# Seven products for eight: Strassen's scheme in the gate and up projections of two fp32 feed-forwards

## The chip, the cores and the metric
The kernel runs on one core of a Trainium2 chip. The metric is the device time of one execution in microseconds; the figure compared is the median over runs. Arithmetic that has to keep fp32 accuracy is done with each fp32 operand split into a rounded part hi and a remainder lo (both of the matmul type fp32r), and three matmuls per product: hi x hi, hi x lo, lo x hi.

## The reference
512 tokens of width 1024 pass two residual blocks (a pooling mixer with a feed-forward, latent attention with a feed-forward), then a third with differential attention and a mixture of experts. The change concerns the two feed-forwards, of hidden width 2816:

```python
def swiglu(h, w_gate, w_up, w_down):
    return (jax.nn.silu(h @ w_gate) * (h @ w_up)) @ w_down
...
    h = rms_norm(x, norm_ffn[i])
    x = x + swiglu(h, ffn_w_gate[i], ffn_w_up[i], ffn_w_down[i])
```

## The kernel before
The tokens lie along the free axis: x is 8 tiles (KT) of 128 channels x 512 tokens, and stays in SBUF. The hidden width is 22 tiles (FT) of 128. `ffn` (L772) takes the hidden tiles in two halves of 11 (HF). For each hidden tile j it takes one weight of 128 x 2048 from the stream (a *pair*: the gate and the up tile), and for gate and up does 8 x 3 matmuls of 512 columns (`mm3`, L519) into one PSUM bank each, 48 in all. The moving operands xh and xl are x times the norm's gain. The norm's factor per token, R, is not in them: it comes late (two hooks after the first pair's two halves make it on VectorE, GpSimd, TensorE and ScalarE), and `evac` (L781) multiplies both PSUM results by R, applies silu, multiplies, and splits the hidden tile into hh and hl. After 11 pairs, 8 down tiles of 11 x 3 matmuls are added to x. The second half's down tiles also call `after(d)`, which prepares the next stage's norm.

The weights come through `Stream` (L82). A queue of DMAs on the SyncE queue fills raw buffers; `split_part` (L193) rounds one 512-column part to hi on ScalarE, and `flush` (L248) does lo = raw - hi, on VectorE, or on GpSimd for parts 2 and 4 (POOLED). The rings have 3 raw, 3 hi and 2 lo buffers of 128 x 2048 (BUFS, L51); a raw buffer is free when its last part is split, hi and lo when `release` says so. In the feed-forwards the order of the work is that of the code: `pump` (L268), called between groups of matmuls, issues the next part's split if there is room, and every engine executes its own instructions in the order issued. The attention stages are issued by a planner with a cost model; the expert stage's order follows the same way.

Four PSUM banks serve as accumulators (`acc`, L488) in rotation. All other tiles are 57 slots of an arena (`tmp`, L485). The two lines on which a pair rests are:

```python
c = slice(k * 256 + m * P, k * 256 + (m + 1) * P)
self.mm3(ps, wh[:, c], wl[:, c], xh[k], xl[k], k == 0, k == KT - 1)
```

In the profile every operation of the planner's engines stands at its helper's line, L357, so names of tiles tell them apart: acc<-xh,hi is a gate or up matmul, acc<-hh,hi a down matmul, lo<-raw,hi a weight's split, t<-acc,R and u<-acc,R an evacuation.

Of the kernel before, what the change touches and what calls it, by code (L numbers as in the profile page):

```python
# [17 lines left out]
P = 128  # L18
T = 512
NT = T // P  # L20
D = 1024
KT = D // P
FF = 2816
FT = FF // P
HF = FT // 2

# [59 lines left out]
class Stream:  # L86
# [16 lines left out]
    def add(self, ap, arena=False):  # L103
        self.items.append(ap)
        self.arena.append(arena)

# [7 lines left out]
    def load(self):  # L114

        nc, tmp = self.net.nc, self.net.tmp
        while self.loaded < len(self.items):
            i, ap = self.loaded, self.items[self.loaded]
            if i >= self.first:
                if not self.load_piece():  # L120
                    return
                continue
            if not self.arena[i]:
                if not self.spare["raw"] or any(self.arena[self.split:i]):
                    return
# [3 lines left out]
                self.raw[i] = self.cut(t, w)  # L129
            else:  # L130
# [62 lines left out]
    def split_part(self):  # L193
        nc, i = self.net.nc, self.split
        if i >= self.first:
            return self.split_piece()
        if self.part == 0:
# [12 lines left out]
        self.half = lo[:, c], r, hi[:, c], i, last  # L210
        if self.part in POOLED[self.phase]:
            self.flush(nc.gpsimd)
        if last:
            self.part = 0
            self.raw.pop(i)
            self.split += 1

    def split_piece(self):
        nc, i, k = self.net.nc, self.split, self.part
# [48 lines left out]
    def pump(self, n=1):  # L268

        plan = self.net.nc  # L270
        for _ in range(n):
            i = self.split
            if i == len(self.items):
                return
            if i < self.first and i >= self.loaded:
                self.flush()
                self.load()
            got = self.raw.get(i, ())
            if self.part >= len(got):
# [20 lines left out]
    def take(self):  # L300
        i = self.taken
        self.taken += 1
        while self.split <= i:
            self.split_part()
        if self.split == i + 1 and self.part == 0:
            self.flush()
        hi, lo, tags = self.out.pop(i)
        w = hi, lo
        self.held.append((w, tags))
        return w  # L310

    def piece(self):

# [161 lines left out]
class Net:  # L475
# [37 lines left out]
    def mm(self, ps, lhsT, rhs, start=True, stop=True):  # L513
        self.nc.tensor.matmul(ps, lhsT, rhs, start=start, stop=stop)
# [254 lines left out]
        sched.spawn(weights(), 0)  # L769


    def ffn(self, l, hooks, after, extra=None):  # L772

        nc = self.nc
        hooks = list(hooks)
        xh, xl = self.held
        for hf in range(2):
            hh, hl = [], []
            pend = []

            def evac(pg, pu):  # L781
                t, u = self.tmp("t"), self.tmp("u")
                nc.vector.tensor_tensor(t, pg, self.R, op=OP.mult)
                nc.scalar.activation(t, t, AF.Silu)
                nc.vector.tensor_tensor(u, pu, self.R, op=OP.mult)
                nc.vector.tensor_tensor(t, t, u, op=OP.mult)
                hh.append(self.tmp("hh", F32R))
                hl.append(self.tmp("hl", F32R))
                self.hilo(hh[-1], hl[-1], t)

            for j in range(HF):
                wh, wl = self.ws.take()
                pp = []
                for m in range(2):
                    ps = self.acc()
                    for k in range(KT):
                        c = slice(k * 256 + m * P, k * 256 + (m + 1) * P)
                        self.mm3(ps, wh[:, c], wl[:, c], xh[k], xl[k], k == 0, k == KT - 1)
                    pp.append(ps)
                    self.ws.pump(2)  # L800
                    if hooks:
                        hooks.pop(0)()
                    elif extra:
                        next(extra, None)
                self.ws.release()
                pend.append(pp)
                if not hooks:
                    while pend:
                        evac(*pend.pop(0))
            for d in range(KT):  # L810
                wh, wl = self.ws.take()
                ps = self.acc()
                for f in range(HF):
                    c = slice(f * P, (f + 1) * P)
                    self.mm3(ps, wh[:, c], wl[:, c], hh[f], hl[f], f == 0, f == HF - 1)
# [5 lines left out]
                if hf == 1:  # L821
                    after(d)

    def ffn_weights(self, l, arena=0):
        for hf in range(2):
            for j in range(HF):
                self.ws.add(self.a["ffn_gu"][l, hf * HF + j], hf * HF + j < arena)
            for d in range(KT):
                self.ws.add(self.a["ffn_dn"][l, hf, d])


    def rope_tables(self):
# [1286 lines left out]
def _host(inp):  # L2119

    f = np.ascontiguousarray
    o = {}
    x = inp["x"][0]
# [5 lines left out]
    def twice(v):  # L2129
# [12 lines left out]
    o["ffn_gu"] = f(gu.reshape(2, 2, KT, P, FT, P).transpose(1, 4, 3, 2, 0, 5)  # L2142
                    .reshape(2, FT, P, 2048))
    o["ffn_dn"] = f(inp["ffn_w_down"].reshape(2, 2, HF, P, KT, P).transpose(0, 1, 4, 3, 2, 5)
                    .reshape(2, 2, KT, P, HF * P))

    wd = inp["mla_w_down"][0]
    wd = np.concatenate([wd, wd[:, 512:]], axis=1)
# [26 lines left out]
    r = np.arange(P)  # L2175
# [4 lines left out]
    c = np.arange(T)[None, :] - 3 * P - r[:, None]  # L2180
# [10 lines left out]
    b = np.zeros((P, 4, 384), np.float32)  # L2191
# [47 lines left out]
```

## Time and profile before

| | |
|---|---|
| median of 3 runs | 1550.54 us (1550.25 to 1555.14) |
| the profiled execution's own time | 1551.3 us |
| its span | 1549.5 us |
| TensorE busy | 1502.5 us, 97% |
| VectorE busy | 946.9 us, 61% |
| ScalarE busy | 753.2 us, 49% |
| GpSimd busy | 397.6 us, 26% |
| weight loads by SyncE's queue | 201.03 MB of 221.57 MB moved |

The two feed-forwards take the stretches from about 36 to 402 us and from about 580 to 945 us; attention, between and after them, and the experts to the end. Busy shares are means over these stages. A matmul's duration in a row is its way through the array, so neighbours overlap: the pace of TensorE is the distance between starts. VectorE's operations overlap a little too. A row's time on GpSimd is rough.

### The profile page before, as it was taken

How to read it: one execution, taken by the hardware profiler on the slowest of the kernel's cores; microseconds unless marked ns; L12 is line 12 of the kernel's file. 1: busy time of each engine (PE TensorE's matmuls, PEld its weight loads, DVE VectorE, ACT ScalarE, POOL GpSimd, SP SyncE). 2: the span in 40 equal slices, each digit the busy share in tenths (PEclk: the TensorE clock that was granted, in tenths of full speed). 3: DMA queues.
4: the chain of work that ended last, by engine and by line, in shares of the span. 5: the costliest groups of instructions: out<-in, count | busy, mean ns of one | idle time of the engine just before them, and what ended most of it. 6: DMA issues, size and time to landing. Idle time of an engine off the chain costs nothing.

```text
span 1549.5 us, 21142 instructions
## 1 busy us (share of the span) xinstructions
PE 1502.5 (97%) x7697; PEld 1222.4 (79%) x7697; DVE 946.9 (61%) x1672; ACT 753.2 (49%) x1553; POOL 397.6 (26%) x314
## 2 busy tenths in 40 slices
PE   8999999999999999999999999999979799999996
PEld 7788888888878888888888889999968666666664
DVE  6464334445387855443444466888986487878774
ACT  5323213223266743232223244787784277777774
POOL 3322123221242113221232123222312222222221
PEclk9999999999999999999999999999979799999999
DMA  6121232223210214313322232212038799999981
GB/s 243 62 104 61 95 135 84 99 73 113 80 63 7 90 62 142 109 57 109 120 97 86 75 111 86 78 57 95 27 112 297 223 312 357 368 366 373 366 295 29
DMA packets 69931, 221.57 MB, mean 143 GB/s; under 512 B 7616, under 2 KB 16960, under 8 KB 56640
## 3 DMA queue, kind: packets, MB, share of 16 engines
q1 hardware_dynamic: 56448, 201.03, 36.5%
q0 software_dynamic: 4064, 14.16, 3.9%
q10 hardware_dynamic: 9312, 5.01, 1.1%
q8 instruction: 61, 1.00, 0.3%
q14 instruction: 46, 0.38, 0.1%
HBM read 208.63 MB, written 11.53 MB: 142 GB/s over the span
## 4 chain that ended last, share of the span: by engine, by line
PE 88%; DVE 5%; ACT 4%; DMA 2%; issue 1%; POOL 0%; ACTq 0%; POOLq 0%; SPq 0%; DVEq 0%
PE acc L357 76%; PE pss L357 8%; PE pst L357 4%; ACT p L357 1%; DVE x L357 1%; DMA bnd<-bands 1%; DVE p L357 1%; DVE xl L357 0%; DVE lo L357 0%; DMA out<-ring,idx 0%; DMA raw<-ffn_gu 0%; ACT hi L357 0%; ACT kl L357 0%; ACT wh L357 0%; ACT kh L357 0%
## 5 line engine op out<-in xcount | busy, mean ns | idle before, releaser
L357 POOL TENSOR_TENSOR lo<-raw,hi 128x512 fp32r<-128x512 f32 (+1 forms) x157 | 224.6, 1440 | 695.9 <-ACT hi L357 593.9
L357 PE MATMUL acc<-xh,hi 128*128 128x512 f32 x744 | 290.5, 390 | 0.5 <-ACT xh L357 0.5
L357 PE MATMUL acc<-xl,hi 128*128 128x512 f32 x744 | 289.6, 389 | 0.3 <-DVE xl L357 0.3
L357 PE MATMUL acc<-xh,lo 128*128 128x512 f32 x744 | 289.5, 389 | 0.0
L357 ACT ACTIVATE hi<-raw 128x512 fp32r<-128x512 f32 (+1 forms) x378 | 208.8, 607 | 86.2 <-issue 59.8
L357 DVE TENSOR_TENSOR wl<-raw,wh 128x512 fp32r<-128x512 f32 x288 | 203.0, 748 | 53.0 <-ACT wh L357 46.8
L357 DVE TENSOR_TENSOR lo<-raw,hi 128x512 fp32r<-128x512 f32 (+1 forms) x221 | 216.5, 989 | 19.8 <-ACT hi L357 19.1
L357 ACT ACTIVATE wh<-raw 128x512 fp32r<-128x512 f32 x320 | 177.5, 621 | 0.0
L357 PEld LDWEIGHTS acc<-xh,hi 128*128 128x128 f32 x744 | 139.7, 188 | 29.8 <-ACT xh L357 0.9
L357 PEld LDWEIGHTS acc<-xl,hi 128*128 128x128 f32 x744 | 139.7, 188 | 29.3 <-DVE xl L357 0.6
L357 PEld LDWEIGHTS acc<-xh,lo 128*128 128x128 f32 x744 | 139.6, 188 | 29.0
L357 DVE TENSOR_TENSOR u<-acc,R 128x512 f32<-128x512 f32 x44 | 30.4, 691 | 181.0 <-PE acc L357 181.0
L357 PE MATMUL acc<-hh,hi 128*128 128x512 f32 x352 | 136.9, 389 | 0.0
L357 PE MATMUL acc<-hl,hi 128*128 128x512 f32 x352 | 136.9, 389 | 0.0
L357 PE MATMUL acc<-hh,lo 128*128 128x512 f32 x352 | 136.9, 389 | 0.0
L357 ACT ACTIVATE hh<-t 128x512 fp32r<-128x512 f32 x44 | 27.8, 632 | 218.4 <-DVE t L357 218.4
L357 DVE TENSOR_TENSOR x<-acc,x 128x512 f32<-128x512 f32 x59 | 40.4, 689 | 119.0 <-PE acc L357 118.9
L357 PE MATMUL acc<-hi,xh 128*128 128x256 f32 x384 | 111.4, 290 | 0.0
L357 PE MATMUL acc<-lo,xh 128*128 128x256 f32 x384 | 109.2, 284 | 0.6 <-DVE lo L357 0.6
L357 PE MATMUL acc<-hi,xl 128*128 128x256 f32 x384 | 109.0, 284 | 0.0
L357 PE MATMUL acc<-wh,teh 128*96 128x512 f32 x224 | 103.1, 460 | 0.2 <-ACT teh L357 0.2
L357 PE MATMUL acc<-wl,teh 128*96 128x512 f32 x224 | 88.1, 393 | 0.8 <-DVE wl L357 0.8
(319 smaller groups left out, 2851.9 us busy)
## 6 DMA issues: line engine op xcount, KB each, us to landing
raw<-moe_w SPq DMA_DIRECT2D x200, 256.0 KB, 8.0
raw<-moe_w SPq DMA_DIRECT2D x46, 1024.0 KB, 11.1
raw<-ffn_gu SPq DMA_DIRECT2D x43, 1024.0 KB, 4.9
raw<-ffn_dn SPq DMA_DIRECT2D x32, 704.0 KB, 4.1
raw<-da_in SPq DMA_DIRECT2D x12, 1024.0 KB, 4.8
raw<-mla_up SPq DMA_DIRECT2D x4, 832.0 KB, 4.4
raw<-mla_o_a SPq DMA_DIRECT2D x12, 256.0 KB, 3.8
raw<-da_o_a SPq DMA_DIRECT2D x12, 256.0 KB, 2.9
```

Source lines behind the costliest of these rows:

```text
L357: r = f(*args, **kw)
```

## The change
Per layer, pairs 0 to 3 stay plain (`plain`) and evacuate as before; from pair 4 on every third is plain on normalized operands (`later`); the other 12 are *summed pairs* (`mixed`). A summed pair computes gate and up for both halves of the tokens at once. With the channels cut into even and odd tiles and the tokens into halves of 256 (H), eight block products become seven of sums (the Winograd form of Strassen's scheme). Each product is 4 x 3 matmuls of 256 columns; two products share a PSUM bank, and VectorE adds the seven results to two hidden halves.

The weight's sums are made in `split_mixed`: of the four 512-column quarters p, q, r, s of the raw tile it needs p, q, p-r side by side with r+s and the like. GpSimd makes two of the four sums and VectorE two; ScalarE rounds seven quarters in four operations, and VectorE subtracts in four (1024, 512, 512 and 1536 columns). The results lie in two groups of hi and lo buffers (products 0 to 3, and 4 to 6). The tokens' sums are made in `mixed_x`, a generator of 4 blocks with 6 steps each, two channel tiles a block: e and o (x times gain times R), their hi and lo, the sums t and e, and their hi and lo. Steps are issued between the matmuls of pairs 1 to 3: two blocks in pair 1, one in the first half of pair 2, one in pair 3.

The hidden tiles are taken in three sets of 8, 7 and 7, with 8 down tiles each, so x is added to three times. Rings: 2 raw, 3 hi, 3 lo. The arrays of weights are laid out anew on the host for this (even before odd tiles). Attention and experts keep their code.

```diff
-HF = FT // 2
+SETS = ((0, 8), (8, 15), (15, 22))
+PLAIN = 4
+EVERY = 3
+H = T // 2
-BUFS = {"raw": 3, "hi": 3, "lo": 2}
+BUFS = {"raw": 2, "hi": 3, "lo": 3}
...
+    def split_mixed(self):
...
+        if step == 0:
+            self.both = self.net.tmp("rs")
+            pool.tensor_tensor(self.both, r, s, op=OP.add)
+            hi(0, 2, pq)
+        elif step == 1:
+            lo(0, 2, pq)
+            pool.tensor_tensor(r, p, r, op=OP.subtract)
+        elif step == 2:
+            hi(3, 1, self.both)
+        elif step == 3:
+            dve.tensor_tensor(p, self.both, p, op=OP.subtract)
+            lo(3, 1, self.both)
+            self.both = None
+        elif step == 4:
+            hi(2, 1, p)
+            dve.tensor_tensor(q, q, p, op=OP.subtract)
+        elif step == 5:
+            lo(2, 1, p)
+            self.ready.append(self.group)
+        elif step == 6:
+            hi(0, 3, qrs)
+        else:
+            lo(0, 3, qrs)
+            self.ready.append(self.group)
...
+    def mixed_x(self, l, full, parts):
...
+        for i in range(KT // 2):
+            e, o, t = self.tmp("xe"), self.tmp("xo"), self.tmp("xt")
+            normed(e, 2 * i)
+            normed(o, 2 * i + 1)
+            yield
+            even, odd = self.pair("b"), self.pair("b")
+            diff(t[:, a], e[:, b], e[:, a], pool)
+            rounded(even[0], e)
+            rounded(odd[0], o)
+            yield
+            diff(t[:, b], o[:, b], t[:, a], pool)
+            diff(even[1], e, even[0].bitcast(F32))
+            diff(odd[1], o, odd[0].bitcast(F32))
+            yield
+            diff(e[:, b], o[:, b], e[:, b])
+            diff(e[:, a], o[:, a], t[:, b])
...
+            for n, (h, c) in enumerate(((even, a), (odd, a), (t12, b), (t12, a), (odd, b),
+                                        (t34, b), (t34, a))):
+                parts[n].append((h[0][:, c], h[1][:, c]))
...
+        def mix_some(n):
+            for _ in range(n):
+                if not hooks and (last or steps[0] < 18):
+                    next(mix, None)
+                    steps[0] += 1
...
+            def product(n, out):
+                nonlocal got
+                if n in (0, 4):
+                    got = self.ws.take_group(n == 4)
+                c = (n % 4) * T
+                for i, (bh, bl) in enumerate(parts[n]):
+                    k = slice(c + i * P, c + (i + 1) * P)
+                    self.mm3(out, got[0][:, k], got[1][:, k], bh, bl, i == 0, i == KT // 2 - 1)
...
+                self.ws.pump()
...
+                if n == 1:
+                    nc.scalar.activation(s1, bank[0], AF.Copy)
+                    add(g0, s1, bank[1])
+                elif n == 3:
+                    add(s0, s1, bank[2])
+                    add(g1, s0, bank[3])
+                    self.ws.pump()
+                elif n == 5:
+                    add(s1, g1, bank[5])
+                    add(g1, g1, bank[4])
+                    add(s0, s0, bank[5])
+                    nc.scalar.activation(g, g, AF.Silu)
+            add(s0, s0, bank[6])
+            nc.vector.tensor_tensor(g, g, s, op=OP.mult)
+            hidden(g)
```

Two engines show how the instructions move at the start of the first layer.

VectorE, from the evacuation of pair 1 on. Before, evacuations and splits alternate, with steps of the rope tables (ang, k) between:

```order
L357 TENSOR_TENSOR t<-acc,R 128x512
L357 TENSOR_TENSOR u<-acc,R 128x512
L357 TENSOR_TENSOR t<-t,u 128x512
L357 TENSOR_TENSOR hl<-t,hh 128x512
L357 TENSOR_TENSOR lo<-raw,hi 128x512
L357 TENSOR_SCALAR k<-ang 128x512
L357 TENSOR_TENSOR lo<-raw,hi 128x512
```

Now there come after the same evacuation block 2 of the normalized tiles (xe, xo, bl), then the first group of pair 4's weight (its lo of 1024 columns, then its sums and their lo):

```order
L447 SCALAR_TENSOR_TENSOR xe<-x,vecs,R 128x512
L447 SCALAR_TENSOR_TENSOR xo<-x,vecs,R 128x512
L447 TENSOR_TENSOR bl<-xe,bh 128x512
L447 TENSOR_TENSOR bl<-xo,bh 128x512
L447 TENSOR_TENSOR xe<-xo,xe 128x256
L447 TENSOR_TENSOR xe<-xo,xt 128x256
L447 TENSOR_TENSOR bl<-xt,bh 128x512
L447 TENSOR_TENSOR bl<-xe,bh 128x512
L447 TENSOR_TENSOR lo<-raw,hi 128x1024
L447 TENSOR_TENSOR raw<-rs,raw 128x512
L447 TENSOR_TENSOR lo<-rs,hi 128x512
```

Behind these stand one more sum and its lo, the evacuation of pair 2 (t, u, t, hl), a lo of 1536 columns (pair 4's second group), and only then block 3 with the same eight rows, the evacuation of pair 3, and the first lo of pair 5. The order in the second layer is the same.

GpSimd at the same place. Before, it has lo splits of parts 2 and 4, and three small things for the rope tables:

```order
L357 TENSOR_TENSOR lo<-raw,hi 128x512
L357 CAST ident_b<-ident 128x128
L357 CAST mask_b<-causal 128x128
L843 DMA pos<-positions 128x512
L357 TENSOR_TENSOR lo<-raw,hi 128x512 x58
```

Now the token sums of block 2 (xt), pair 4's two weight sums, then those of block 3 and of pair 5:

```order
L447 TENSOR_TENSOR xt<-xe 128x256
L447 TENSOR_TENSOR xt<-xo,xt 128x256
L447 TENSOR_TENSOR rs<-raw 128x512
L447 TENSOR_TENSOR raw<-raw 128x512
L447 TENSOR_TENSOR xt<-xe 128x256
L447 TENSOR_TENSOR xt<-xo,xt 128x256
L447 TENSOR_TENSOR rs<-raw 128x512
L447 TENSOR_TENSOR raw<-raw 128x512
```

So pair 4's weight sums stand before the last block's token sums on GpSimd, and pair 5's right behind them; the rope tables' work comes after both.

On TensorE 24 pairs of 48 matmuls become 24 of 84, in seven runs of twelve. In all 2016 matmuls of 256 columns stand in place of 1152 of 512.

## Rows read from the trace of the kernel before
**Rows 1.** The page, its first part: busy time, share of the span, instructions.
```profile
PE 1502.5 (97%) x7697; PEld 1222.4 (79%) x7697; DVE 946.9 (61%) x1672; ACT 753.2 (49%) x1553; POOL 397.6 (26%) x314
```
**Rows 2.** The chain in order of time, both feed-forwards: start us, us, what.
```profile
51.09 348.21 PE acc L357 x1536
...
591.61 353.59 PE acc L357 x1581
```
**Rows 3.** Windows, a stretch of the first feed-forward: us, each engine's busy, PEclk, DMA.
```profile
100.00:150.00 50.00, 50.00 (x222) 41.41 (x221) 25.56 (x32) 15.07 (x27) 12.30 (x9) 1.00 0.26 86
```
**Rows 4.** Timeline of TensorE, differential attention: start us, us, instruction; first and last.
```profile
964.89 0.28 PE L357 MATMUL acc<-hi,xl 128*128 128x256 f32 x1
...
973.28 0.28 PE L357 MATMUL acc<-lo,xh 128*128 128x256 f32 x1
```
**Rows 5.** Timeline of VectorE, start of the first feed-forward; idle and releaser in brackets.
```profile
51.76 0.69 DVE L357 TENSOR_TENSOR t<-acc,R 128x512 f32<-128x512 f32 x1 [6.95 <-ACT R L357]
...
55.70 0.68 DVE L357 TENSOR_TENSOR lo<-raw,hi 128x512 fp32r<-128x512 f32 x1
...
62.38 0.68 DVE L357 TENSOR_TENSOR t<-acc,R 128x512 f32<-128x512 f32 x1
62.98 0.68 DVE L357 TENSOR_TENSOR u<-acc,R 128x512 f32<-128x512 f32 x1
...
65.77 0.69 DVE L357 TENSOR_TENSOR lo<-raw,hi 128x512 fp32r<-128x512 f32 x1
66.37 1.52 DVE L357 TENSOR_SCALAR k<-ang 128x512 f32<-128x512 f32 x1
67.81 1.78 DVE L357 TENSOR_TENSOR lo<-raw,hi 128x512 fp32r<-128x512 f32 x1
```
**Rows 6.** Timeline of VectorE, pooling mixer: a scalar_tensor_tensor and the next start.
```profile
28.61 0.74 DVE L357 SCALAR_TENSOR_TENSOR x<-acc,vecs,x 128x512 f32<-128x512 f32 x1
29.27 0.74 DVE L357 SCALAR_TENSOR_TENSOR xl<-x,vecs,xh 128x512 fp32r<-128x512 f32 x1
```
**Rows 7.** Groups by line and form: operation, count, busy us, mean ns, idle before.
```profile
L357 DVE TENSOR_TENSOR t<-t,u 128x512 f32<-128x512 f32 x44 | 30.5, 693 | 5.7 <-ACT t L357 1.3
...
L357 DVE TENSOR_TENSOR on<-acc,on 128x256 f32<-128x256 f32 x16 | 6.7, 419 | 7.4 <-ACT on L357 7.3
...
L357 ACT ACTIVATE hi<-raw 128x512 fp32r<-128x512 f32 x342 | 194.6, 620 | 86.2 <-issue 59.8 <-PE acc L357 15.8 <-DMA raw<-ffn_dn 5.5
...
L357 POOL TENSOR_TENSOR lo<-raw,hi 128x512 fp32r<-128x512 f32 x153 | 222.6, 1465 | 686.0 <-ACT hi L357 584.0 <-PE acc L357 66.9 <-issue 21.3
...
L357 POOL TENSOR_TENSOR lo<-raw,hi 128x128 fp32r<-128x128 f32 x4 | 2.0, 501 | 9.9 <-ACT hi L357 9.9
```
**Rows 8.** DMA issues: KB each, median us from issue to landing.
```profile
raw<-ffn_gu SPq DMA_DIRECT2D x43, 1024.0 KB, 4.9
```
**Rows 9.** Timelines of GpSimd and of VectorE beside it, first feed-forward.
```profile
66.25 2.80 POOL L357 TENSOR_TENSOR lo<-raw,hi 128x512 fp32r<-128x512 f32 x2 [5.68 <-ACT hi L357]
...
141.54 3.01 POOL L357 TENSOR_TENSOR lo<-raw,hi 128x512 fp32r<-128x512 f32 x2 [8.15 <-ACT hi L357]
...
141.96 1.43 DVE L357 TENSOR_TENSOR lo<-raw,hi 128x512 fp32r<-128x512 f32 x1 [0.27 <-ACT hi L357]
143.65 0.69 DVE L357 TENSOR_TENSOR t<-acc,R 128x512 f32<-128x512 f32 x1 [0.26 <-PE acc L357]
```
**Rows 10.** Windows, end of the differential attention, columns as in rows 3.
```profile
1130.00:1135.00 5.00, 3.06 (x14) 2.79 (x15) 3.55 (x13) 4.11 (x11) 0.00 (x0) 0.75 0.00 0
...
1140.00:1145.00 5.00, 1.62 (x7) 1.09 (x7) 4.31 (x12) 4.85 (x12) 0.70 (x1) 0.77 0.51 157
1145.00:1150.00 5.00, 3.83 (x17) 3.05 (x16) 3.24 (x11) 5.00 (x15) 0.00 (x0) 0.50 0.01 2
1150.00:1155.00 5.00, 4.36 (x14) 3.85 (x14) 4.89 (x13) 4.97 (x13) 1.28 (x1) 0.50 0.72 211
```

More of the change, by code (lines that the diff above doesn't have):

```diff
@@ L101, in __init__, with add @@
         self.hold, self.gate, self.phase = False, None, 0
-    def add(self, ap, arena=False):
+        self.mixed, self.group, self.both, self.ready = {}, None, None, []
+    def add(self, ap, arena=False, mixed=False):
+        if mixed:
+            self.mixed[len(self.items)] = None
         self.items.append(ap)
@@ L216, in split_part, with group, hi, lo @@
             self.split += 1
+    def group(self, i):
+        th, tl = self.room()
+        return self.tile("hi", F32R, th), self.tile("lo", F32R, tl), (th, tl)
+    def split_mixed(self):
+        nc, i, step = self.net.nc, self.split, self.part
+        dve, pool = nc.vector, nc.gpsimd
+        if step == 0:
+            self.flush()
+            if i >= self.loaded:
+                self.load()
+        if step in (0, 6):
+            self.group = self.room()
+            self.group = (self.tile("hi", F32R, self.group[0]),
+                          self.tile("lo", F32R, self.group[1]), self.group)
+        p, q, r, s = self.raw[i]
+        t = self.mixed[i]
+        def hi(k, n, src):
+            c = slice(k * self.PART, (k + n) * self.PART)
+            nc.scalar.activation(self.group[0][:, c], src, AF.Copy)
+        def lo(k, n, src):
+            c = slice(k * self.PART, (k + n) * self.PART)
+            dve.tensor_tensor(self.group[1][:, c], src, self.group[0][:, c].bitcast(F32),
+                              op=OP.subtract)
+        pq, qrs = t[:, :2 * self.PART], t[:, self.PART:4 * self.PART]
+        self.part += 1
+        if step == 0:
+            self.both = self.net.tmp("rs")
[21 more added lines that the diff above has]
+            self.ready.append(self.group)
+            self.group = None
+            self.raw.pop(i)
+            self.mixed[i] = None
+            self.split += 1
+            self.flushed += 1
+            self.spare["raw"] += 1
+            self.part = 0
+            self.load()
     def split_piece(self):
@@ L278, in pump @@
             got = self.raw.get(i, ())
+            if i in self.mixed:
+                if not got or self.part in (0, 6) and not self.room():
+                    return
+                self.split_part()
+                continue
             if self.part >= len(got):
@@ L310, in take, with take_group @@
         return w
+    def take_group(self, last):
+        while not self.ready:
+            self.split_part()
+        hi, lo, tags = self.ready.pop(0)
+        self.held.append(((hi, lo), tags))
+        self.taken += last
+        return hi, lo
     def piece(self):
@@ L776, in ffn @@
         xh, xl = self.held
[L777 to L793, printed above, removed]
-                for m in range(2):
[L795 to L800, printed above, removed]
+        parts = [[] for _ in range(7)]
@@ new lines, in ffn, with plain, mm @@
+        steps = [0]
+        def plain(last):
+            wh, wl = self.ws.take()
+            pp = []
+            def mm(m, k, begin, end):
+                o = (2 * m + k % 2) * T + k // 2 * P
+                c = slice(o, o + P)
+                self.mm3(pp[m], wh[:, c], wl[:, c], xh[k], xl[k], begin, end)
+            def mix_some(n):
[3 more added lines that the diff above has]
+                        steps[0] += 1
+            if last:
+                pp += [self.acc(), self.acc()]
+                for k in range(KT):
+                    for m in range(2):
+                        mm(m, k, k == 0, k == KT - 1)
+                    xh[k] = xl[k] = None
+                    if k > 1:
+                        mix_some(1)
+                    if k % 2:
+                        self.ws.pump(2)
+            else:
+                for m in range(2):
+                    pp.append(self.acc())
+                    for n, k in enumerate((0, 2, 4, 6, 1, 3, 5, 7)):
+                        mm(m, k, n == 0, n == KT - 1)
+                        if n % 4 < 3:
+                            mix_some(1)
+                    self.ws.pump(3)
@@ L801, in ffn, with hidden @@
                     if hooks:
                         hooks.pop(0)()
-                    elif extra:
-                        next(extra, None)
[L805 to L809, printed above, removed]
+            self.ws.release()
+            pend.append(pp)
+            if not hooks:
+                while pend:
+                    evac(*pend.pop(0))
+        def hidden(t):
+            hh.append(self.tmp("hh", F32R))
+            hl.append(self.tmp("hl", F32R))
+            self.hilo(hh[-1], hl[-1], t)
@@ new lines, in later @@
+        def later():
+            wh, wl = self.ws.take()
+            pp = []
+            for m in range(2):
+                ps = self.acc()
+                for n, k in enumerate((0, 2, 4, 6, 1, 3, 5, 7)):
+                    o = (2 * m + k % 2) * T + k // 2 * P
+                    c = slice(o, o + P)
+                    self.mm3(ps, wh[:, c], wl[:, c], *full[k], n == 0, n == KT - 1)
+                    if n % 2:
+                        self.ws.pump()
+                pp.append(ps)
+            self.ws.release()
+            t = self.tmp("t")
+            nc.scalar.activation(t, pp[0], AF.Silu)
+            nc.vector.tensor_tensor(t, t, pp[1], op=OP.mult)
+            hidden(t)
@@ L810, in ffn @@
+        for f0, f1 in SETS:
+            hh.clear()
+            hl.clear()
+            for j in range(f0, f1):
+                if j < PLAIN:
+                    plain(j == PLAIN - 1)
+                    if j == PLAIN - 1:
+                        for _ in mix:
+                            pass
+                elif self.plain(j):
+                    later()
+                else:
+                    mixed()
             for d in range(KT):
@@ L812, in ffn @@
                 ps = self.acc()
-                for f in range(HF):
+                n = f1 - f0
+                for f in range(n):
                     c = slice(f * P, (f + 1) * P)
-                    self.mm3(ps, wh[:, c], wl[:, c], hh[f], hl[f], f == 0, f == HF - 1)
+                    self.mm3(ps, wh[:, c], wl[:, c], hh[f], hl[f], f == 0, f == n - 1)
                     if f % 3 == 1:
```

73 lines of the change are left out of this document (65 added, 8 removed).

## The prediction
> **What bounds the kernel now.** I read the page first: TensorE is busy 97% of the span, VectorE 61%, ScalarE 49%, GpSimd 26% [rows 1]. Then the chain of waits in order of time: it runs through the first feed-forward as one piece of 348.21 us with 1536 matmuls and through the second as one of 353.59 us with 1581 [rows 2]. Nothing is waited for in either, so only less TensorE work or a new wait can move these stages. 348.21 / 1536 gives 226.7 ns for a 512-wide matmul. Then the window of one such stretch: the granted clock is 1.00, its upper level of 2.4 GHz, and VectorE is half idle, 25.56 of 50 us [rows 3]. I take the price of a 256-wide matmul, each with its own 128x128 weights, from the timeline of the differential attention: 71 in a row start between 964.89 and 973.28, 70 steps in 8.39 us, so 119.9 ns [rows 4].
>
> **The gain on TensorE.** Call the pairs 0 to 21 in each layer; pairs 4, 5, 7, 8, 10, 11, 13, 14, 16, 17, 19 and 20 become summed pairs. Before, a pair is 48 matmuls x 226.7 = 10.88 us. A summed pair is 7 products x 4 x 3 = 84 matmuls x 119.9 = 10.07 us. 24 pairs save 24 x 0.81 = **19.4 us**. The other 20 pairs and the down products keep their matmuls.
>
> A page speaks against this. By the Trainium skill ("TensorE: Matmul & The Clock Gate", section Back-to-back issue gap) matmuls that each load weights come every 81 ns at 128 columns and every 131 ns at 512; read linearly that is 98 ns at 256, an estimate, and a pair would go from 6.3 to 8.2 us, 46 us worse over 24. Rows 2 and 4 do not agree: here halving the width nearly halves the spacing.
>
> **What it adds beside TensorE.** The prices for VectorE are start-to-start times. A 512-wide operation takes 0.60 (62.38 to 62.98), a scalar_tensor_tensor 0.66 (28.61 to 29.27) [rows 5, 6]; 256 columns take 0.27 less (419 against 693 ns) [rows 7], so 0.33, and I extrapolate 1.14 and 1.69 for 1024 and 1536. The evacuation of a plain pair takes 3.39 with its waits for ScalarE (62.38 to 65.77), the first of a layer 3.94 (51.76 to 55.70) [rows 5].
>
> *A summed pair in the steady state.* Splitting its weights: 1.14 + 4 x 0.60 + 1.69 = 5.2; evacuating: 7 x 0.33 + 2 x 0.60 = 3.5; in all 8.7 of 10.07 us, and at most 2.4 more for two 512-wide GpSimd operations (below). The third pair of each three is a plain one with about 4. The first group of the next pair is ready some 8 to 9 us into a pair and needed at 10.07. I cost this at nothing, with one microsecond of cover; without it, 12 second pairs of a couple would stall.
>
> *Down products in three sets.* Eight more x additions a layer (0.60 each) beside tiles of 21 or 24 matmuls, 4.76 or 5.44 us, which hold about 2.4 of VectorE: nothing. The last chain of a set (multiply, round, subtract) ends near 2.7 us after its products; the first tile needs it after 18 matmuls, 4.08 us: nothing. In each layer's last set the normalization adds 1.9 to 2.5 to each 4.76 us tile; with a GpSimd collision that is about 5. If late, it is late by under 1 us per layer at the start of the next stage.
>
> *Ring 2/3.* A raw tile lands 4.9 us after its issue [rows 8] and is asked for a pair, over 10 us, ahead; the number of buffers is the same. Nothing, with 2 us either way for the attention, whose planned order shifts a little.
>
> *The start of each layer*, where the change decides. The normalized tiles and their sums (four blocks) cannot start before R, when VectorE also has the plain evacuations, and VectorE takes its queue in order. The order printed with the change shows what lies before the last block: a whole summed weight. I add it up from 55.70 in the first layer, without any collision: blocks 0 to 2, each 2 x 0.66 + 4 x 0.60 + 2 x 0.33 plus some 0.4 of waits for ScalarE (0.62 a rounding, rows 7) = 4.8, so 14.4; two lo of pair 3, 1.2; evacuations of pairs 1 and 2, 6.8; first group of pair 4, 1.14 + 4 x 0.60 + 0.6 waits = 4.1; its second group, 1.69 + 0.9 = 2.6; block 3 up to its first lo, 2.0. That is 31.1, so 86.8. TensorE starts pair 1 at 51.09 [rows 2], pair 4 at 51.09 + 3 x 10.88 = 83.7, and has used up blocks 0 to 2 of the first product 9 x 0.12 = 1.1 later, at 84.8. Even the lower bound is **2.0 late**. Pair 5 then waits for its weights: behind block 3 (to 89.6) stand the evacuation of pair 3 (3.4) and 5.2 us of splits and evacuations of pair 4, to 98.2, while TensorE ends pair 4 at 95.8: 2.4 more. Lower bound **4.4 us a layer**.
>
> Now GpSimd. Where it runs, a VectorE operation on two SBUF inputs lasts until the GpSimd operation is over: the lo at 141.96 took 1.43 beside a GpSimd pair that began at 141.54, the k and lo beside the pair of 66.25 took 1.52 and 1.78; an evacuation from PSUM took its usual 0.69 [rows 5, 9]. So a 512-wide GpSimd operation costs VectorE up to 1.2, and a 256-wide one, between 501 ns at 128 columns and 1465 at 512 (a mean with collisions in it) [rows 7], some 0.6. Up to the first lo of block 3 these are the eight xt sums (seven in time), one lo of pair 3 and the two 512-wide sums of pair 4: 4.1 + 1.2 + 2.5 = 7.8, so it is ready at 94.6, 9.8 late. Behind it three more collisions (3.1) put the last lo of block 3 at 100.5. TensorE gets through the third product at about 100.2, then four more of 1.44: pair 4 ends at 105.9 for 93.8. Pair 5 can start 8.6 after 100.5, at 109.1: 3.2 more. Upper bound **15.3 us a layer**. Some GpSimd operations will fall into VectorE's waits for ScalarE; most, since VectorE is never idle here, will not. I take **12**, nearer the rows with a collision.
>
> The second layer repeats it (same offset from R to pair 1, same order): 24 us for two, bounds 8.8 and 30.6.
>
> *Clock.* TensorE would stand idle 5 to 9 us at pair 4. In the last part of the differential attention, after TensorE was busy 3.06 of 5 us in one window and 1.62 in another, the grant stood at 0.50 (the lower level, 1.2 GHz) to past 1155 [rows 10]. Where that happens, work up to the third product is hidden by the same wait; four products behind it could take twice 1.44. I take 1 us a layer, bounds 0 and 5.7.
>
> **Sum.** -19.4 + 24 + 2 = **+6.6 us** on the profiled execution's own 1551.3: 1557.9. The median shown, 1550.54, is 0.8 below, so I predict **1557 us**. 0.3% of it, 4.65 us, is about what a measurement can tell from no change.
>
> **Rivals.**
> - *GpSimd fits into the gaps (faster).* Place: blocks 0 to 3 in each layer; price: 4.4 us a layer instead of 12. For it: blocks have hand-offs to ScalarE, and evacuations read PSUM. Against: rows 5 and 9. Sum -19.4 + 8.8 = -10.6, so 1540. The other side begins where the delay is under 7.4 a layer; that asks that GpSimd costs VectorE no more than a quarter of what rows 5 and 9 show. Chance of faster by over 0.3%: 0.32, for I may also have counted an operation's price or a queue place too dearly.
> - *A middle: no change.* Delay 7.4 to 12 us a layer: 1546 to 1555. Chance 0.24.
> - *Stalls go on past the start.* If the steady state's one microsecond of cover is gone (rope tables add up to two VectorE operations to each of the first seven summed pairs), each of 12 couples stalls 0.5 to 1 us, and with the slow clock at both starts: +6.6 + 9 = 1566 and up to 1573. For it: 8.7 + 2.4 is over 10.07. Against: the plain pair in each three catches up. Chance 0.10.
> - *My forecast itself*, 1555 to 1563: 0.34.
>
> Slower by over 0.3% is the last two, 0.44. The range runs from the faster rival, 1541, to the middle of the stalling one, 1569.
>
> **What would show it.** Right: matmuls acc<-bh,hi 128x256 every 0.12 us in pairs 10 and later; TensorE idle behind VectorE's bl near 85 to 95 us, and again before pair 5 behind a lo; the same in the second layer near 625; lo and bl of 1.2 us and more while GpSimd runs; the chain naming VectorE bl. The second half of each feed-forward without waits. Wrong: a first summed pair without a gap (then 19 us are gained), gaps at every second summed pair, a spacing of 256-wide matmuls away from 0.12, or a feed-forward whose length did not move by -10 + 12 us.

## The result, and the profile after

The changed kernel takes 1566.56 us, median of 4 runs (1565.13 to 1567.43); the kernel before, run beside it, 1551.59 (1550.25 to 1555.14). The ratio is 1.0092, with a 95% interval of 1.0072 to 1.0112: 15.0 us slower, where 6.5 were forecast (1557 on the 1550.54 shown; the sum itself has 6.6 on the profiled execution). The profiled execution took 1566.71 us, its span is 1564.9.

The page of the changed kernel, first part; it answers to [rows 1]:
```profile
PE 1497.2 (96%) x8561; PEld 1258.0 (80%) x8561; DVE 1087.6 (69%) x1928; ACT 817.5 (52%) x1609; POOL 433.0 (28%) x346
```
TensorE has 5.3 us less busy time, though the span is 15.4 us longer, so TensorE now waits, and part of its busy time is slow. The chain of waits of the changed kernel in order of time (start us, us, what) answers to [rows 2]:
```profile
94.60 307.49 PE acc L447 x1814
...
582.32 4.80 DMA raw<-ffn_gu
...
588.48 0.76 DVE xl L447
...
590.94 7.17 PE acc L447 x24
...
661.48 295.64 PE acc L447 x1735
```
The single pieces of [rows 2] began at 51.09 and 591.61, with pair 1. Now an unbroken piece begins only at 94.60 and 661.48. Ahead of the first, the timeline of TensorE shows three waits (idle time and releaser in brackets):
```profile
83.62 0.39 PE L447 MATMUL acc<-xh,lo 128*128 128x512 f32 x1
86.95 0.55 PE L447 MATMUL acc<-bh,hi 128*128 128x256 f32 x1 [2.95 <-DVE t L447]
...
88.80 0.41 PE L447 MATMUL acc<-bh,lo 128*128 128x256 f32 x1
93.52 0.58 PE L447 MATMUL acc<-bh,hi 128*128 128x256 f32 x1 [4.31 <-ACT bh L447]
94.60 0.58 PE L447 MATMUL acc<-bl,hi 128*128 128x256 f32 x1 [0.49 <-DVE bl L447]
94.97 0.41 PE L447 MATMUL acc<-bh,lo 128*128 128x256 f32 x1
```
The first is for a PSUM bank: VectorE evacuates pair 2 (t at 86.12) only behind the first group of pair 4's split. The others are for block 3 of the normalized tiles. VectorE's timeline shows what held both:
```profile
86.12 0.68 DVE L447 TENSOR_TENSOR t<-acc,R 128x512 f32<-128x512 f32 x1
...
90.32 1.76 DVE L447 TENSOR_TENSOR lo<-raw,hi 128x1536 fp32r<-128x1536 f32 x1 [0.68 <-ACT hi L447]
92.00 0.75 DVE L447 SCALAR_TENSOR_TENSOR xe<-x,vecs,R 128x512 f32<-128x512 f32 x1
...
93.50 1.04 DVE L447 TENSOR_TENSOR bl<-xe,bh 128x512 fp32r<-128x512 f32 x1
...
95.60 1.49 DVE L447 TENSOR_TENSOR xe<-xo,xe 128x256 f32<-128x256 f32 x1
...
99.27 0.69 DVE L447 TENSOR_TENSOR bl<-xe,bh 128x512 fp32r<-128x512 f32 x1
```
Block 3 starts at 92.00, behind the whole split of pair 4. And the windows of that stretch (columns as in [rows 3]) show the granted clock behind the waits:
```profile
80.00:85.00 5.00, 4.01 (x18) 3.00 (x16) 4.54 (x7) 2.67 (x4) 0.44 (x1) 1.00 0.00 0
85.00:90.00 5.00, 2.26 (x9) 1.99 (x9) 3.79 (x7) 2.40 (x4) 0.00 (x0) 0.63 0.00 0
90.00:95.00 5.00, 0.98 (x3) 0.69 (x4) 4.58 (x5) 1.55 (x3) 2.10 (x2) 0.50 0.39 108
95.00:100.00 5.00, 5.00 (x25) 5.00 (x25) 4.94 (x6) 1.26 (x2) 4.92 (x6) 0.51 0.24 102
100.00:105.00 5.00, 5.00 (x44) 5.00 (x44) 3.83 (x6) 3.00 (x5) 0.10 (x1) 1.00 0.18 52
```
The grant falls to 0.50, the lower level, and stays there until about 100: 25 matmuls in the fourth window, 44 in the fifth.

The second layer has waits of the same kind at pair 4 (3.56, 4.81 and 0.50 us), and one more in pair 5, behind VectorE's work on the router's table wr (VectorE, then TensorE):
```profile
659.42 0.33 DVE L447 TENSOR_TENSOR wr<-wr,vecs 128x160 f32<-128x160 f32 x1 [1.46 <-DMA wr<-router]
659.67 1.75 DVE L447 TENSOR_TENSOR lo<-raw,hi 128x1536 fp32r<-128x1536 f32 x1
...
661.48 0.38 PE L447 MATMUL acc<-bh,lo 128*128 128x256 f32 x1 [1.45 <-DVE lo L447]
```

To see where the 15 us are, I cut each profiled execution where the second half of a layer's first pair begins (44.61 and 585.11 before), at the first long TensorE piece of the attention's products (407.07) and in the differential attention (950.75). "Rest" is from there to the end of the span.

| us | first feed-forward | attention | second feed-forward | rest | median of runs (before beside it) |
|---|---|---|---|---|---|
| before | 362.46 | 178.04 | 365.64 | 598.75 | |
| the change | 365.01 | 181.08 | 371.72 | 602.24 | 1566.56 (1551.59) |
| e1 rings 3/2 | 375.68 | 178.00 | 385.98 | 602.30 | 1587.14 (1551.18) |
| e2 five plain | 358.80 | 181.90 | 365.99 | 598.16 | 1552.00 (1551.18) |
| e3 none summed | 371.13 | 181.29 | 374.79 | 597.06 | 1572.22 (1551.18) |
| e4 sums moved | 363.59 | 180.97 | 367.53 | 602.31 | 1559.55 (1551.18) |
| e5 no lending | 364.87 | 183.10 | 369.68 | 597.32 | 1561.46 (1552.84) |
| e6 block first | 365.12 | 181.98 | 372.34 | 600.30 | 1566.76 (1552.84) |
| e7 all | 358.10 | 182.09 | 360.17 | 600.02 | 1548.40 (1552.84) |
| e8 all, 30 pairs | 360.34 | 183.11 | 359.77 | 597.60 | 1549.58 (1552.84) |
| e9 xt moved | 364.75 | 181.02 | 370.84 | 600.06 | 1565.23 (1551.20) |
| e10 five, xt | 359.33 | 182.15 | 361.24 | 602.60 | 1549.98 (1551.20) |
| e11 six, xt | **354.12** | 182.06 | **357.98** | 604.37 | **1542.69** (1551.20) |
| e12 six, 28 pairs | 356.26 | 181.13 | 356.93 | 599.41 | 1541.91 (1551.79) |

The rest holds the same work in the changed kernel as before, yet differs by 7 us between executions. Most of that lies in one stretch, from the 24-matmul piece ahead of the router to the experts' first piece of 20 matmuls (1194.45 to 1267.45 before): it took 73.00 us before, 76.79 in the change, 79.32 in e11 and 71.88 in e5, at a mean granted clock of 0.88, 0.84, 0.83 and 0.91. Why the grant differs there stays open. So a change of one stage is read from its own column, and 3.5 of the 15.4 us between the two profiled executions are not shown to be the change's.

### The profile page after: what moved, and what is told of

The parts are those of the page before. It is cut to its first block, busy times and chain, and to the rows that moved or that the text cites. A ratio compares the mean times of both kernels' runs of the same rounds, so it can differ in the third digit from the quotient of the medians.

```text
span 1564.9 us, 23422 instructions
## 1 busy us (share of the span) xinstructions
PE 1497.2 (96%) x8561; PEld 1258.0 (80%) x8561; DVE 1087.6 (69%) x1928; ACT 817.5 (52%) x1609; POOL 433.0 (28%) x346
## 4 chain that ended last, share of the span: by engine, by line
PE 81%; DVE 8%; ACT 6%; DMA 2%; issue 2%; ACTq 0%; POOL 0%; POOLq 0%; SPq 0%; DVEq 0%
PE acc L447 69%; PE pss L447 8%; PE pst L447 4%; DVE lo L447 2%; DVE xe L447 1%; ACT hi L447 1%; DVE bl L447 1%; ACT p L447 1%; DMA raw<-ffn_gu 1%; DMA bnd<-bands 1%; DVE xl L447 1%; DVE t L447 1%; ACT bh L447 1%; DVE p L447 1%; DVE x L447 0%
## 5 line engine op out<-in xcount | busy, mean ns | idle before, releaser
L447 ACT ACTIVATE hi<-raw 128x512 fp32r<-128x512 f32 (+2 forms) x354 | 236.0, 697 | 209.1 <-PE acc L447 100.9
L447 POOL TENSOR_TENSOR lo<-raw,hi 128x512 fp32r<-128x512 f32 (+2 forms) x125 | 166.0, 1334 | 599.5 <-ACT hi L447 574.5
L447 PE MATMUL acc<-bh,hi 128*128 128x256 f32 (+1 forms) x864 | 268.0, 310 | 15.6 <-ACT bh L447 9.1
L447 PE MATMUL acc<-bh,lo 128*128 128x256 f32 (+1 forms) x864 | 267.5, 310 | 1.4 <-DVE lo L447 1.4
L447 PE MATMUL acc<-bl,hi 128*128 128x256 f32 (+1 forms) x864 | 267.8, 310 | 1.0 <-DVE bl L447 1.0
L447 DVE TENSOR_TENSOR lo<-raw,hi 128x512 fp32r<-128x512 f32 (+2 forms) x229 | 230.4, 1007 | 26.6 <-ACT hi L447 25.8
L447 PEld LDWEIGHTS acc<-bh,hi 128*128 128x128 f32 x864 | 167.5, 194 | 24.8 <-ACT bh L447 9.7
L447 PEld LDWEIGHTS acc<-bh,lo 128*128 128x128 f32 x864 | 167.5, 194 | 9.4 <-DVE lo L447 1.8
L447 PEld LDWEIGHTS acc<-bl,hi 128*128 128x128 f32 x864 | 167.5, 194 | 9.4 <-DVE bl L447 1.8
L447 PE MATMUL acc<-wh,tel 128*96 128x512 f32 x224 | 88.5, 395 | 0.0
```

Source lines behind the costliest of these rows:

```text
L447: r = f(*args, **kw)
```

## The experiments

Each starts from the changed kernel unless it says otherwise.

**e1: rings of 3 and 2 again.**
```
-BUFS = {"raw": 2, "hi": 3, "lo": 3}
+BUFS = {"raw": 3, "hi": 3, "lo": 2}
```


> The changed kernel with its raw ring put back to 3 and its lo ring to 2; nothing else. In the changed kernel's trace the first gate/up load of the second layer's ring starts at 582.32 us, when the last output product of the attention stage frees the ring; ScalarE's next instruction waits for it until 587.21, with the last xh behind it, and the first pair then runs 7.17 us for a half in place of 5.61. Theory (the ring of 2 costs this): both go, about 4.8 + 1.5 = 6 us, so 1560.5 us (1559 to 1562). Rival 1 (the ring costs nothing, the wait would have come anyway behind the norm): 1566.5 us, within 1.5. Rival 2 (two lo buffers are too few for summed pairs, whose groups each hold one until the fourth or the seventh product): waits of some 0.5 us in each of 24 pairs, 1572 us or more.

Measured: 1587.14 us, ratio to before 1.0218 (1.0198 to 1.0237). The attention is back at 178.00 and the first pair's half at 5.61 us, as the theory says; but both feed-forwards lose more than that, as rival 2 says. TensorE's waits in the first, from 51 to 330 us (in total, times, longest):
```profile
PE acc L447 <- DVE lo L447: 10.7, 8, 2.7
PE acc L447 <- ACT hi L447: 1.7, 2, 1.0
```
So the ring of two raw buffers costs 3 us in the attention, and with the wait there goes the slow first pair (1.6 us). The waits for lo fit rival 2, that summed pairs need the third lo buffer; but the edit moves both rings at once, and three buffers of each were not tried.

**e2: five plain pairs.**
```
-PLAIN = 4
+PLAIN = 5
```


> The changed kernel with five plain pairs at the start of each layer in place of four; the number of summed pairs stays 24. Theory (the wait ahead of the first summed pair is VectorE's backlog at the start of the layer, some 10 us of work more than four pairs leave time for, and the half clock follows from it): one pair more gives VectorE 10.9 us, the wait falls from 9.4 us to under 2 us a layer and the half clock behind it goes too, together 20 to 24 us, so 1545 us (1542 to 1552). Rival (the block of sums is tied to the last plain pair, so the wait only moves by one pair): 1566 us, within 3, with the same idle time one pair later.

Measured: 1552.00 us, ratio 1.0003 (0.9990 to 1.0016): 14.6 us less than the change, the same as before. What is left of the waits in the first feed-forward behind 95 us:
```profile
PE acc L447 <- ACT bh L447: 2.0, 1, 2.0
PE acc L447 <- DVE bl L447: 0.9, 2, 0.8
```
VectorE starts block 3 at 96.07 in place of 92.00: one plain pair moves TensorE's need 10.9 us back and the block only 4.1. The backlog is real, but one pair does not clear it; the 2 us a layer expected to be left were too few: with 12 summed pairs gaining 0.763 us each (e11), the first layer still loses 358.80 - 362.46 + 9.16 = 5.5.

**e3: no summed pair, the rest as changed.**
```
-EVERY = 3
+EVERY = 1
...
+                if extra:
+                    next(extra, None)
```
(The added lines go into the plain pair's function, which now has to drive the tables.)


> The changed kernel with no summed pair: every pair behind the first four takes its eight products from the normalised operands, which are made with their sums as before; sets, rings and the start of the layer stay. It computes the whole feed-forward. Theory (a summed pair takes 84 products of 119.9 ns for 48 of 226.7 ns and runs without waits, so each saves 0.81 us of path, and the loss is all at the start): 24 x 0.81 = 19.4 us slower, less what the fourth pair no longer waits, 1580 to 1587 us. Rival (summed pairs gain little, since waits between their products take it back): 1560 to 1570 us.

Measured: 1572.22 us, ratio 1.0139 (1.0116 to 1.0161). The time lies between the two theories. The two feed-forwards alone are 9.2 us over the change's (745.92 against 736.73), the rest 5.2 under. Since nothing is summed, +8.7 and +9.2 us a feed-forward against before are what normalized tiles, sets and rings cost by themselves; the summed pairs take back 6.1 and 3.1 of it. I had taken the start to cost the same with and without them; that was wrong.

**e4: sums on VectorE.**
```
-            pool.tensor_tensor(self.both, r, s, op=OP.add)
+            dve.tensor_tensor(self.both, r, s, op=OP.add)
...
-            pool.tensor_tensor(r, p, r, op=OP.subtract)
+            dve.tensor_tensor(r, p, r, op=OP.subtract)
...
-            diff(t[:, a], e[:, b], e[:, a], pool)
+            diff(t[:, a], e[:, b], e[:, a])
```
The text on record says all sums; the edit left four of the eight xt differences of a layer on GpSimd.


> The changed kernel with all sums and differences on VectorE that it puts on GpSimd: four of 128x256 a layer's start and two of 128x512 a summed pair. Theory (much of VectorE's backlog at the start is time in which its operations run at 1.2 to 1.8 us beside a GpSimd operation in place of 0.7): VectorE gets some 4 x 0.35 + 4 x 0.7 = 4 us more work ahead of the first summed pair, and loses some 8 us of stretching, so the wait there shortens by 2 to 6 us a layer: 1556 to 1563 us. Rival (the backlog is VectorE's own work and the stretching small): 3 to 5 us more a layer, 1572 to 1577 us.

Measured: 1559.55 us, ratio 1.0052 (1.0033 to 1.0070), within the theory's range. The second feed-forward is 4.2 us shorter than the change's 371.72, of which 1.6 are the first pair, which here ran at the upper clock; the first is 1.4 shorter.

**e9: the eight xt differences alone on VectorE** tells which of the moved sums mattered.
```
-            diff(t[:, a], e[:, b], e[:, a], pool)
+            diff(t[:, a], e[:, b], e[:, a])
...
-            diff(t[:, b], o[:, b], t[:, a], pool)
+            diff(t[:, b], o[:, b], t[:, a])
```


> The changed kernel with all eight differences of 128x256 (xt) that a layer's start puts on GpSimd on VectorE; the sums of the weights stay on GpSimd. The run with the sums on VectorE had moved only four of these eight. Theory (a GpSimd operation of 1.1 to 2 us stretches what VectorE does beside it, and VectorE also waits for its result): VectorE gets 8 x 0.35 = 2.8 us of work and loses more than that, so the wait ahead of the first summed pair shortens by 1 to 4 us a layer: 1559 to 1564 us. Rival (these differences cost nothing on GpSimd; what helped there was the weights' sums): 1567 to 1572 us.

Measured: 1565.23 us, ratio 1.0088 (1.0074 to 1.0101); the feed-forwards fall by 0.3 and 0.9. That is between the two expectations: less than the theory's 1 to 4 a layer, more than the rival's nothing. The operation of 1.49 us above took 0.42 here, so VectorE was stretched less there, but it gained little more by that than it paid in work. Most of what e4 gained thus came with the weights' sums, though the two edits differ in more than those. How much of the wait GpSimd causes would be told by a run without these sums on any engine, which wasn't tried.

**e5: no lending of the raw ring at the end of the first attention.** `lend` is the index behind the second layer's first pair.
```
-            if not spare[tag] and self.arena[self.split]:
+            if not spare[tag] and self.arena[self.split] and self.split >= self.lend:
```


> The changed kernel, in which no half of an output product of the first attention stage may take a buffer of the raw ring for itself: the first ring load of the second layer no longer waits for those products. Theory (with two raw buffers the fourth product's two halves hold the whole ring until the stage's last matmul at 582.27 us; the kernel before lends one to the third and two to the fourth, so that its first load goes out at 566.56): the stretch between the layers falls from 181.1 us to the 178.0 of before, and the first pair's half from 7.17 to 5.6 us, together 3 to 4.6: 1562 to 1563.6 us. Rival (the half that finds no buffer is cut later and TensorE waits for it instead): 1566 us or more, with the wait earlier in the stage.

Measured: 1561.46 us, ratio 1.0067 (1.0052 to 1.0083). The median is 0.5 us under the theory's range, but not for its reason: the attention took 183.10, not 178.0. TensorE's waits from 400 to 600 us, in which the two differ, first the change's, then e5's:
```profile
PE acc L447 <- ACT xh L447: 1.3, 1, 1.3
...
PE acc L447 <- DVE xl L447: 0.3, 1, 0.3
```
```profile
PE acc L447 <- ACT oh L447: 1.4, 1, 1.4
...
PE acc L447 <- DVE ol L447: 0.3, 1, 0.3
```
The load is no longer waited for and the first pair's half is 5.61 us, but TensorE now waits for ScalarE's oh at 514.83, in a chain with a split of weights on ScalarE (hi at 509.60) ahead of it, and the grant falls there, as the windows show, first the change's, then e5's:
```profile
515.00:520.00 5.00, 4.17 (x23) 3.27 (x21) 5.00 (x13) 4.48 (x13) 1.12 (x1) 1.00 0.19 71
```
```profile
515.00:520.00 5.00, 4.70 (x15) 3.51 (x16) 4.02 (x9) 2.35 (x7) 1.30 (x1) 0.50 0.00 2
```
This is the rival's mechanism, the wait only moved. From the first pair to the end of the second feed-forward this execution is only 0.2 us shorter than the change's; the rest is 4.9 us shorter, so the lower time is not shown to be the edit's.

**e6: block 3 ahead of the rest of the split.**
```
-                    self.ws.pump(3)
+                    self.ws.pump(3 if len(hh) < PLAIN - 3 else 2)
...
-                        mix_some(1)
-                    if k % 2:
+                        mix_some(3)
+                    if k > 2:
```


> The changed kernel with the fourth block of sums ahead of the rest of the first summed pair's split in VectorE's order (after the first two steps of that split instead of all eight); the work is the same. Theory (the wait ahead of the first summed pair is a matter of VectorE's order: 0.69 + 0.69 + 1.76 us of the split stand ahead of the block whose results TensorE wants first): the block ends some 3 us sooner, the half clock behind the wait shortens with it, 3 to 4 us a layer: 1558 to 1561 us. Rival (VectorE's total of work is what counts, and the lo halves that now stand behind the block are wanted as soon): the wait moves to a lo and the time stays at 1566 us, within 2.

Measured: 1566.76 us, ratio 1.0097 (1.0083 to 1.0112): the rival. TensorE's waits in the second feed-forward:
```profile
PE acc L447 <- DVE lo L447: 9.6, 3, 7.4
```
The wait has gone from block 3 to the lo that now stands behind it. In the first feed-forward a wait for block 3 stayed (2.8 us in place of 4.3), with one of 1.9 us for a weight's hi. Neither became shorter (365.12 and 372.34): what VectorE has to do ahead of pair 4 counts here, not this part of its order.

**e7: five plain pairs with the edits of e4, e5 and e6, and the router's tables loaded half a pair before use.** As in e4, four xt differences a layer stay on GpSimd.
```
+        self.wr = c.tile([P, KT, 20], F32, name="wr")
+        nc.scalar.dma_start(out=self.wr, in_=a["router"])
...
+        yield
         yield
         self.moe_tables()
```


> Five plain pairs, all sums and differences on VectorE, the fourth block ahead of the rest of the split, no lending of the raw ring at the end of the first attention stage, and the router's tables loaded half a pair before they are used; 24 summed pairs. Theory (what the change cost is all in these places): the start of a layer loses under 2 us, the stretch between the layers is that of before, the router's wait is gone, and of the 19.4 us gain some 14 to 19 are left against the kernel before: 1534 to 1539 us. Rival (24 summed pairs with all their sums on VectorE, 1.2 us more a pair, outrun their cover): waits in the summed pairs, 1545 us or more.

Measured: 1548.40 us, ratio 0.9973 (0.9963 to 0.9983), 9 us over the theory. The chain of e7 names VectorE in the summed pairs themselves, piece behind piece:
```profile
105.78 0.60 DVE rs L447
106.39 1.14 DVE lo L447
107.52 0.60 DVE raw L447
108.12 0.33 DVE t L447
108.45 0.60 DVE raw L447
109.06 0.60 DVE lo L447
```
With the weights' sums there, VectorE is the bound for whole pairs: the rival. TensorE's waits in its products come to 2.3 us in the first feed-forward and 2.8 in the second; another 4 us are the attention's, which did not return to that of before (182.09 for 178.04).

**e8: the same with 30 summed pairs.**
```
-EVERY = 3
+EVERY = 6
```


> The kernel of the run before with a plain pair only after every five summed ones, so 30 summed pairs. Theory (a summed pair takes VectorE about 10 us or more of TensorE's 10.07 with its sums there, and the plain pairs between are what lets it catch up): waits of some 1 us in the third to fifth pair of each run take the 6 x 0.81 = 4.9 us back and more, so the same time as the run before or up to 8 us slower. Rival (VectorE still has slack): 4.9 us faster than the run before.

Measured: 1549.58 us, ratio 0.9982 (0.9973 to 0.9992): six summed pairs more gain nothing, as the theory says.

**e10: five plain pairs, the edits of e5 and e9, the early tables.** Order and weights' sums are the change's again.


> Five plain pairs, the eight differences on VectorE, the weights' sums on GpSimd, the split in the changed kernel's order, no lending of the raw ring at the end of the first attention stage, and the router's tables loaded half a pair before their use; 24 summed pairs. Theory (the run with all in one was held by VectorE's sums for the weights in its summed pairs and by the block put ahead of the split; without both, only some 3 us a layer of the start are left): 1541 to 1546 us. Rival (GpSimd's sums stretch VectorE as much as they spare it): 1547 to 1551 us.

Measured: 1549.98 us, ratio 0.9987 (0.9976 to 0.9999), inside the rival's range. The waits of the first feed-forward still hold block 3:
```profile
PE acc L447 <- ACT bh L447: 2.1, 1, 2.1
PE acc L447 <- DVE bl L447: 0.9, 1, 0.9
```

**e11: e10 with six plain pairs.**
```
-PLAIN = 5
+PLAIN = 6
```


> The kernel of the run before with six plain pairs and 22 summed ones. Theory (what is left at the start is VectorE's backlog, which one pair more of 10.9 us clears): 2 x 0.81 = 1.6 us slower for the two pairs and some 3 us a layer faster at the start: 2 to 5 us under the run before. Rival (nothing is left at the start): 1.6 us over it.

Measured: 1542.69 us, ratio 0.9940 (0.9927 to 0.9954): faster than before by 8.5 us, and than e10 by 7.3, more than expected, though two pairs fewer are summed. The chain of e11 has the first feed-forward in one piece again:
```profile
51.06 339.82 PE acc L447 x1932
```
Block 3 and two of its results in VectorE's timeline of e11:
```profile
101.07 0.75 DVE L447 SCALAR_TENSOR_TENSOR xe<-x,vecs,R 128x512 f32<-128x512 f32 x1
...
105.33 0.78 DVE L447 TENSOR_TENSOR bl<-xe,bh 128x512 fp32r<-128x512 f32 x1
...
106.63 0.41 DVE L447 TENSOR_TENSOR xe<-xo,xe 128x256 f32<-128x256 f32 x1
```
Six plain pairs end at 51.06 + 5 x 10.88 = 105.5, block 3 is wanted 1.1 us behind that, and its first lo is there by 106.1.

**e12: e11 with 28 summed pairs** (EVERY 6).


> The kernel of the run before (six plain pairs) with a plain pair only after every five summed ones: 28 summed pairs in place of 22. Theory (with the weights' sums on GpSimd a summed pair leaves VectorE 0.9 us of 10 idle, so five in a row run without waits): 6 x 0.81 = 4.9 us under the run before, 1537 to 1539 us. Rival (VectorE's backlog from the plain pairs' evictions and splits has no pair to go down in): waits inside the runs of summed pairs that take the 4.9 us back, 1542 us or more.

Measured: 1541.91 us, ratio 0.9940 (0.9926 to 0.9953): between the two expectations, and the same as e11. The attention and both feed-forwards are 894.3 us, in e11 894.2. Three more summed pairs should make the first feed-forward 2.3 us shorter than e11's; it is 2.1 longer. Its longest waits name part of what takes the gain back:
```profile
PE acc L447 <- DVE lo L447: 2.4, 2, 1.3
```

## Why the prediction came out as it did

**The gain on TensorE was right.** The unbroken piece of e11 holds 11 summed pairs: 339.82 against 348.21 us of [rows 2], 8.39 less, so 0.763 a pair for a forecast of 0.81. Its 924 narrow matmuls take 339.82 - 1008 x 0.2267 = 111.3 us, 120.5 ns each, for 119.9 from [rows 4]. 24 pairs gain 18.3 us, not 19.4. The rule weighed there, of the Trainium skill ("TensorE: Matmul & The Clock Gate", section Back-to-back issue gap), gave an estimate of 98 ns for 256 columns; e11's number does not agree.

**The steady state was right.** From 94.60 on, the first feed-forward of the change has no wait; 2 of 3 pairs summed fit VectorE. e7, e8 and e12 show how narrow that is: two more 0.60 us operations of VectorE a pair, or five summed pairs in a row, and TensorE waits.

**The start of a layer was right in size, by luck in part.** With the measured gain, the first layer lost 365.01 - 362.46 + 12 x 0.763 = 11.7 us, for 12 + 1 forecast; the second 15.2. The queue tally that counted every GpSimd collision gave 94.6 for the first lo of block 3 and 100.5 for the last: they ended at 93.50 + 1.04 = 94.54 and 99.96. But the step "Pair 5 then waits for its weights", 2.4 to 3.2 us, failed: there is no such wait. A product needs only its own quarters of a group and not the whole: pair 5 began at 105.92, behind the lo of its first 1024 columns and ahead of the group's other two lo, which ended at 106.47 and 108.47. The rows, VectorE and then TensorE:
```profile
103.72 1.23 DVE L447 TENSOR_TENSOR lo<-raw,hi 128x1024 fp32r<-128x1024 f32 x1 [0.26 <-ACT hi L447]
...
105.92 0.28 PE L447 MATMUL acc<-bh,hi 128*128 128x256 f32 x1
```
And "Clock", 1 us a layer, was too small: of the 11.7 us, 2.95 + 4.31 + 0.49 = 7.75 are idle, and the other 4.0 are matmuls at the lower level, before the second wait and up to 100 us. Some of the slow stretch may hide what VectorE still has to make; no run shows how much. The wait for a PSUM bank was not foreseen; it lies ahead of the larger one, which would, by VectorE's order, have been there without it. The wait put too high and the clock put too low cancel: that the sum comes near 12 + 1 is luck, the time of block 3 is not.

**What made the sum's 6.6 into 15 us** were two terms priced at nothing, and the rest.
- "Ring 2/3" ("Nothing, with 2 us either way for the attention"): 3.0 us in the attention (181.08 for 178.04) and 7.17 - 5.61 = 1.6 in the first pair. The step counted buffers, not who else takes them: with two, the fourth output product's halves hold both raw buffers until the stage's last matmul, the load waits until 582.32, and ScalarE's in-order queue holds xh behind the split of that load. e1 shows that the 3.0 us are the ring's; e5, that letting go of it earlier only moves the wait. The 1.6 us are the clock behind that wait and do not always come: e3 and e4 have the same ring and waits, and 5.57 and 5.59 us.
- The router's tables moved from pair 1 (their load is issued at 595.0 us before) into pair 5, the second summed one (657.7); I had not listed that step. In the second layer a 1.45 us wait followed, since VectorE's wr, issued right behind its load, stands ahead of a lo. e10 and e11, which load them earlier, have no such wait. In e9 VectorE waits 1.60 us for the same load and TensorE does not: it costs only where VectorE has no lead.
- Rest: +3.5 us in the profiled execution, with unchanged work; not shown to be the change.

Together -18.3 + (11.7 + 15.2, less the 1.6 and 1.45 in it) + 4.6 + 1.45 + 3.5 + 0.2 at the kernel's start = 15.3, for a difference of spans of 15.4.

**The rivals.** GpSimd did not fit into the gaps, and stalls did not go on past the start; the slower outcome came from the boundary instead. 1566.56 lies outside the forecast's own 1555 to 1563 and where the stalling rival put it, without that rival's mechanism: that the range still holds the time is luck.

## What to carry to other kernels

A saving in the steady state is worth what its preparation leaves of it: here 18.3 us were gained and more lost in the first 60 us of each layer, and two more plain pairs a layer, with their 10.9 us each for VectorE (and the small edits of e10), turned +15 into -8.5 us against before. Tally the in-order queue of the helper engine up to the first use, item by item; that tally was right to 0.1 us for the first result wanted and 0.5 for the last. When ring sizes are traded, list everything that may take a buffer, not only the loads.

## What the hardware showed beyond that

- A break of 2.95 us in TensorE's work was followed by matmuls every 0.213 us in place of 0.120, and the lower level lasted through 25 matmuls behind the third wait: 4.0 us on top of 7.75 idle. At the second layer's first pair, waits of 1.26 and 0.29 us came with 7.17 us in place of 5.61 in the change, and without that loss in e4, whose waits were 1.17 and 0.28, and in e3, whose waits were 1.37 and 0.29.
- A 256-wide VectorE difference took 1.49 us beside a 512-wide weight's sum on GpSimd and 0.41 without; still, taking GpSimd's eight 256-wide differences away and giving them to VectorE gained only 0.3 and 0.9 us a layer.
- 600 us of unchanged work differ by 7 us between executions (597.06 to 604.37), more than most effects studied here, and the longer ones had the lower granted clock in one stretch of 72 to 79 us.
